# Memory attention of the sample group in the projection, and all sums of output weights made during the prompt attention

## The chip, the cores and the metric

The kernel runs on one core of one Trainium2 chip. The metric is device time in microseconds (us); before the change the median of three runs is 2398.44 us (2398.2 to 2399.28). The execution that was profiled took 2395.7 us.

## The reference

One mixer layer (DEPTH = 1) is computed for a prompt of 2048 tokens and for a sample group of 8 sequences with 4 new tokens each, from shared weights. All data is f32.

```python
D_MODEL, SEQ, DEC_BATCH, DEC_SEQ = 1024, 2048, 8, 4
SB_HEADS, SB_HEAD_DIM, MEM_HEADS, MEM_HEAD_DIM, N_MEM = 8, 64, 4, 128, 256
# h = rms_norm(x);  z = h @ w_in, split into column groups
# A  conv:   GLU -> causal depthwise conv (31) -> LayerNorm -> swish -> pointwise
# B  pool:   causal means over 2/4/8/16 minus the token, small matmul, scale
# C  stick-breaking attention: a = beta_k * prod over later k' of (1 - beta_k'), out = a @ v
# D  cross-attention into 256 memory tokens: softmax(q k^T / sqrt(128)) @ v
# each group output * silu(its gate);  concat @ w_out;  rms_norm;  + x
```

The change concerns group D of the sample group (its keys and values come from `cache_mem_k` and `cache_mem_v`, 256 tokens by 512 columns for each of the 8 sequences) and the product with `w_out` (2048 x 1024).

## The kernel before

**Stages.** There are three, one after the other on the tensor engine (PE):

- The *projection* (until about 1478 us) computes `z = h @ w_in` in two halves of the columns, part 0 and part 1. Every f32 operand is split into a high and a low fp32r piece, and three products are summed (`xhi*whi`, `xlo*whi`, `xhi*wlo`, L243). Beside it, PE works through the stick-breaking attention of the sample group on the paged cache (L987, L1026), whose pages GpSimd (POOL) fetches by indirect DMA (L941). Side tasks are added to `tasks` in `main` (L1865) and give PE a little work between the products.
- The *prompt attention* (`sb_prompt`, L1293, about 1478 to 1937 us) runs over `hp` (4 pairs of heads), `qb` (4 blocks of 512 queries) and `kc` (blocks of 512 keys from `qb` down to 0). For each block, PE makes scores `S` (L1271); ScalarE (ACT) makes two sigmoids, `gam` (L1275) and `be` (L1276); VectorE (DVE) scans `E` (L1341, L1344); POOL multiplies `be` by `E` (L1353); PE transposes the result into `AT` (L1364); DVE or ACT copies it to `at` (L1368 on the diagonal, L1370 elsewhere); PE multiplies it with `V` into `av` (L1380). The scan's second operand `ZM` is in PSUM (L1300, L1905).
- The *output stage* (about 1937 to 2394 us) computes `concat @ w_out` with a Strassen-like scheme of seven products, in the order 1, 7, 2, 6, 4, 5, 3 (`parts`). Each product takes eight weight tiles of 128x512. For products 7, 6, 5 and 4 such a tile is a sum or difference of blocks of `w_out`, made on POOL (`weight_sum`, L1615). Then ACT makes the high piece (`wohi`, L1621), DVE the low one (`wolo`, L1626; POOL for product 1). On the other side, blocks of the mixer output `mr` are combined (L1699 to L1706) and split into `mh` and `ml` (L1714, L1725). PE accumulates them into `acc` (L1968). The tail of the conv group (`conv_post`, L1444 to L1514: layer norm, swish, pointwise product `cz` at L1511 from `shi` and `slo`, gate `cgt` at L1514) is interleaved there.

**Group D of the sample group.** `sample_keys` (L440) runs as a task in part 0: for each of 8 sequences it loads the keys, transposes them on PE (`smt`, L453), copies them from PSUM on ACT (L454) and stores them to `mkTd` in DRAM. `sample_mem` (L1147) runs as the first side work of the prompt attention: it loads them again (`mkbT`, L1174) with the values (`mvb`, L1168), makes scores `smS` (L1181), a softmax, transposes of the probabilities (`smpt`, L1205), products with the values (`smO`, L1220), picks each head's columns with a mask (`smOm` and `smR` on DVE, L1223 and L1227), transposes back (`smr`, L1231) and stores its part of the mixer output (L1237). `sample_end` (L1079 to L1144) finishes the sample group's stick-breaking attention behind it.

**What sets the order.** PE's order is written by hand (`manual_schedule`): a block's transposes follow its scores by a fixed number of steps, and side work is taken between steps by a budget of cost. The orders of ACT, DVE, POOL and of the DMA issues on SyncE (SP) are made by a tile scheduler when the program is built, which may hoist an instruction far ahead of where the source has it. Each engine executes its own order strictly; an instruction whose input isn't ready holds up all behind it on its engine.

`side_work` (L1927) is the list of what is done beside the prompt attention: `sample_mem`, `sample_end`, the weights of product 1 (`out_weights`, L1629), the first mixer blocks, and the start of the conv tail. In the output stage, `out_weights(prod, pool, engine, lead, ...)` loads weight tiles `lead` steps ahead of their use.

## Time and profile before

| what | value |
|---|---|
| median of 3 runs | 2398.44 us (2398.2 to 2399.28) |
| profiled execution | 2395.7 us, its span 2394.0 us |
| PE busy | 2275.1 us (95%) |
| DVE, POOL, ACT busy | 1732.6, 1286.6 and 1117.0 us (72%, 54% and 47%) |
| mean granted PE clock | 0.986 |
| DMA traffic | 562.14 MB, mean 235 GB/s |

The span is the time between the first and the last instruction on record; the execution's own time is 1.7 us longer. The times of stages are read in us from the span's start. A row of a waits view has the waiting engine and line, what released it, and total, count and longest of these waits. In a timeline row stand start, duration, engine, line, operation and tiles, and in brackets the idle time of the engine ahead of it with its releaser. In a windows row, each engine's busy time within the stretch is followed by the number of its instructions; then come granted clock, busy share of the DMA engines, and GB/s.

### The profile page before, as it was taken

What the parts mean: (1) busy time and instruction counts of PE and PEld (TensorE: products, weight loads), DVE (VectorE), ACT (ScalarE), POOL (GpSimd) and SP (SyncE); (2) the same over time, 40 slices, a digit from 0 to 9 for tenths busy, and PEclk for the clock granted to TensorE, in tenths of its full rate; (3) what the DMA queues carried; (4) which work ended last, traced back from release to release, by engine and by line L of the source; (5) the groups of instructions that cost most, each with busy time, mean ns of one, the idle gap of its engine ahead of it and who ended that gap; (6) DMA issues with size and microseconds to landing.
All of it is one profiled execution on the core that took longest, in us unless ns stands there. A gap on an engine that the chain in (4) does not pass through costs nothing. (4 is left out here: it accounts for less than half of the span.)

```text
span 2394.0 us, 42116 instructions
## 1 busy us (share of the span) xinstructions
PE 2275.1 (95%) x15962; PEld 1769.7 (74%) x15962; DVE 1732.6 (72%) x2420; ACT 1117.0 (47%) x1939; POOL 1286.6 (54%) x1323
## 2 busy tenths in 40 slices
PE   7899999999999999999999999899999998989996
PEld 7888888898888777777777776455555557778775
DVE  5332785959756764587877878879898846687998
ACT  5322343242442322224242435788989955443554
POOL 3454535556464655546556554667776754454430
PEclk9999999999999999999999999999999999999998
DMA  6678988887778899978878767834333217887764
GB/s 211 196 253 290 347 287 309 305 269 267 259 256 306 301 357 318 318 270 276 272 268 274 260 222 190 238 77 119 82 93 80 63 63 250 268 284 239 255 236 164
DMA packets 340437, 562.14 MB, mean 235 GB/s; under 512 B 28481, under 2 KB 212929, under 8 KB 323834
## 3 DMA queue, kind: packets, MB, share of 16 engines
q1 hardware_dynamic: 284858, 290.72, 39.2%
q0 software_dynamic: 55376, 268.72, 31.6%
q8 instruction: 126, 2.06, 0.3%
q14 instruction: 77, 0.63, 0.1%
HBM read 469.28 MB, written 90.68 MB: 234 GB/s over the span
## 5 line engine op out<-in xcount | busy, mean ns | idle before, releaser
L974 DVE STREAM_TRANSPOSE T<-kt 128x1024 f32<-128x1024 f32 x256 | 308.5, 1225 | 184.1 <-PE sSA L987 179.4
L941 POOL DMA_INDIRECT vt<-in_cache_v_dram,idv x256 | 252.8, 988 | 255.1 <-PE sO L1026 194.3
L629 DVE SCALAR_TENSOR_TENSOR cacc<-U,par,cacc 128x512 f32<-128x512 f32 x480 | 360.2, 750 | 11.5
L1353 POOL TENSOR_TENSOR be<-be,E 128x512 f32<-128x512 f32 (+3 forms) x316 | 301.2, 960 | 106.1 <-DVE E L1344 45.9
L1344 DVE TENSOR_TENSOR_SCAN E<-gam,cr,ZM 128x513 f32<-128x513 f32 x192 | 233.0, 1264 | 14.8 <-ACT gam L1275 13.5
L941 POOL DMA_INDIRECT kt<-in_cache_k_dram,idk x128 | 128.1, 1001 | 194.3 <-DVE T L974 155.0
L1364 PEld LDWEIGHTS AT<-ident,be 128*128 128x128 f32 x1082 | 115.7, 141 | 128.1 <-ACT at L1370 45.1
L1968 PE MATMUL acc<-wohi,mh 128*128 128x512 f32 (+1 forms) x480 | 194.6, 405 | 2.1 <-DVE mh L1725 1.1
L1275 ACT ACTIVATE gam<-S,nbias_bc 128x1024 f32<-128x1024 f32 (+1 forms) x158 | 171.6, 1086 | 46.0 <-ACT be L1276 17.1
L1968 PE MATMUL acc<-wolo,mh 128*128 128x512 f32 (+1 forms) x480 | 190.8, 397 | 0.0
L1968 PE MATMUL acc<-wohi,ml 128*128 128x512 f32 x448 | 179.0, 400 | 9.8 <-DVE ml L1725 9.6
L1271 PE MATMUL S<-kT,Q 128*128 128x512 f32 (+1 forms) x632 | 175.2, 401 | 4.6 <-DVE sg1sg L727 2.4
L1276 ACT ACTIVATE be<-S,bias_bc 128x1024 f32<-128x1024 f32 (+1 forms) x158 | 170.7, 1080 | 0.0
L1364 PE MATMUL AT<-ident,be 128*128 128x128 f32 x1082 | 156.3, 282 | 15.0 <-DVE at L1368 3.9
L1380 PE MATMUL av<-at,V 128*64 128x512 f32 (+3 forms) x640 | 152.6, 555 | 1.7 <-DVE sbo L1385 1.7
L987 PE MATMUL sSA<-T,W 128*32 128x128 f32 x4096 | 138.4, 276 | 3.2 <-DVE T L974 2.4
L987 PEld LDWEIGHTS sSA<-T,W 128*32 128x32 f32 x4096 | 104.1, 110 | 40.0 <-issue 31.1
L1725 DVE TENSOR_TENSOR ml<-mr,mh 128x512 fp32r<-128x512 f32 x108 | 98.6, 918 | 35.0 <-ACT mh L1714 34.6
L1026 PE MATMUL sO<-vt,saT 128*32 128x512 f32 x1024 | 122.3, 593 | 0.0
L1271 PEld LDWEIGHTS S<-kT,Q 128*128 128x128 f32 x632 | 105.6, 194 | 19.7 <-ACT be L1276 3.4
L1370 ACT COPY at<-AT 128x512 f32<-128x512 f32 x192 | 109.5, 661 | 14.4 <-PE AT L1364 14.4
L1341 DVE TENSOR_TENSOR_SCAN E<-gam,ZM 128x384 f32<-128x384 f32 (+1 forms) x124 | 94.5, 812 | 24.8 <-ACT gam L1275 22.1
(581 smaller groups left out, 6044.3 us busy)
## 6 DMA issues: line engine op xcount, KB each, us to landing
Q<-qd SPq DMA_DIRECT2D x64, 256.0 KB
mr<-mixd SPq DMA_DIRECT2D x32, 512.0 KB
mr<-mixd SPq DMA_DIRECT2D x48, 256.0 KB
wor<-in_w_out_dram SPq DMA_DIRECT2D x20, 512.0 KB
xtp<-in_x_prompt_dram SPq DMA_DIRECT2D x16, 512.0 KB
kT<-kd SPq DMA_DIRECT2D x64, 128.0 KB
wor<-in_w_out_dram SPq DMA_DIRECT2D x32, 256.0 KB
msd<-mr SPq DMA_DIRECT2D x32, 256.0 KB
```

Of the source, the lines that this page charges most:

```text
L629: dve.scalar_tensor_tensor(out=ps, in0=U[:, a + k : a + k + H], scalar=wd[:, k : k + 1], in1=ps, op0=ALU.mult, op1=ALU.add)
L941: pool.indirect_dma_start(out=dst, out_offset=None, in_=rows, in_offset=bass.IndirectOffsetOnAxis(ap=idx, axis=0))
L974: S["turn"] = dve.transpose(T[:, 2 * hh : 2 * hh + 2].rearrange("p s j t -> p (s j t)"), kt[:, 2 * hh : 2 * hh + 2].rearrange("p s j d -> ...
L987: pe.matmul(sSs[n][32 * g : 32 * g + 32, P * ml : P * (ml + 1)], lhsT=W[:, jj, :], rhs=T[:, :, jj, :], start=i == 0, stop=i == 3, tile_pos ...
L1271: pe.matmul(S[:, j, :w], lhsT=Q[:, x, P * (q2 + j) : P * (q2 + j + 1)], rhs=kt[:, :w], start=x == 0, stop=x == 1)
L1275: act.activation(out=ga, in_=S[:, :, :w], func=AF.Sigmoid, bias=nbias_bc[:, h : h + 1], scale=-1.0)
L1276: act.activation(out=be, in_=S[:, :, :w], func=AF.Sigmoid, bias=bias_bc[:, h : h + 1])
L1344: dve.tensor_tensor_scan(out=E[:, j][:, ::-1], data0=g_[:, j][:, ::-1], data1=ZM[:, 0:1].to_broadcast([P, 513]), initial=carry[hh, q2][:, ...
L1353: pool.tensor_tensor(out=be[:, j, :m], in0=be[:, j, :m], in1=E[:, j, 513 - w : 513 - w + m], op=ALU.mult)
L1364: pe.transpose(ap_[:, P * qt : P * (qt + 1)], A[hp, qb, kc, hh, qt][:, P * r : P * (r + 1)], ident)
L1380: pe.matmul(av[64 * hh : 64 * hh + 64, c], lhsT=V[:, 4 * kc + r, 64 * hh : 64 * hh + 64], rhs=ats.pop((hp, qb, kc, r, hh))[:, c], start=dg ...
L1968: pe.matmul(o[:rows], lhsT=m[a][:, k, :rows], rhs=W[prod, 4 * h + k][w], start=not cont and h == k == n == 0, stop=h == 1 and k == 3 and n ...
```

## The change

Three things are changed.

1. `sample_keys`, its DRAM tile `mkTd` and the round trip through it are gone. `sample_mem` becomes a task of the projection's part 1. For each sequence it loads the keys, transposes them (8 transposes), copies them on ACT, and makes the scores at once (4 matmuls of 32x256, one to each strip of 32 columns of the array); DVE adds the result into `sc`. Then follow the softmax and, for each sequence, 4 matmuls with the values, a copy on ACT, and two small matmuls with a selection matrix `Sel` that pick the heads and transpose at once, in place of `smOm`, `smR` and `smr`.
2. The side work of the prompt attention now begins with `sample_end`. Behind it comes `weight_sums`: for each of 8 steps two loads of 512 KB, four sums of 128x512 on POOL and two stores of 512 KB to `wsd`. The weights of product 1 come after it.
3. In the output stage `weight_sum` is gone: products 7, 6, 5 and 4 load ready sums from `wsd`, two tiles in one transfer, and products 7 and 5 load two steps ahead in place of one.

```diff
-    mkTd = dram.tile([NB, P, 4, NMEM], F32, name="mkTd")
-    wsd = dram.tile([2, 8, P, 512], F32, name="wsd")
+    wsd = dram.tile([2, 8, P, 2, 512], F32, name="wsd")
...
-    def sample_keys():
-        for b in range(NB):
...
-            sp.dma_start(k_, cmk[b].rearrange("(t p) c -> p t c", p=P))
...
-            wq.dma_start(mkTd[b], kT)
...
+    def sample_mem():
+        while state["early"] < 6:
+            yield
...
+        ahead = yield from rows(cmk, 0, "mkb")
...
         for b in range(NB):
+            k_ = ahead
+            ahead = yield from (rows(cmk, b + 1, "mkb") if b + 1 < NB else rows(cmv, 0, "mvb"))
+            kT = k4(f"mkbT{b}", [P, 4, NMEM], F32)
+            for t in range(2):
+                pt = tp_tile(f"smt{b}_{t}")
...
+                    pe.transpose(pt[:, P * h : P * (h + 1)], k_[:, t, P * h : P * (h + 1)], ident)
+                act.copy(kT[:, :, P * t : P * (t + 1)], pt.rearrange("p (h n) -> p h n", h=4))
+                yield
+            yield
+            S = tp_tile(f"smS{b}")
+            for h in range(4):
+                pe.matmul(S[32 * h : 32 * h + 32, :NMEM], lhsT=qm[:, b, h, :], rhs=kT[:, h, :], start=True, stop=True,
+                          tile_position=(0, 32 * h))
+            if b:
                 dve.tensor_tensor(out=sc, in0=sc, in1=S[:, :NMEM], op=ALU.add)
...
+        for b in range(NB):
+            k, g = divmod(b, 4)
...
+            O = tp_tile(f"smO{b}")
             for t in range(2):
+                for c in range(2):
+                    r = 64 * t + 32 * c
+                    pe.matmul(O[r : r + 32, :256], lhsT=pv[:, t, g], rhs=v_[:, t, 256 * c : 256 * c + 256], start=True,
+                              stop=True, tile_position=(0, r))
+            Os = small(f"smOs{b}")
+            act.copy(Os[:, :256], O[:, :256])
...
+            for n in range(2):
+                pe.matmul(pt[:, 2 * TS * n : 2 * TS * (n + 1)], lhsT=Os[:, P * n : P * (n + 1)],
+                          rhs=Sel[:, k, n].rearrange("p c q -> p (c q)"), start=True, stop=True)
...
         sp.dma_start(mixs[3], mo)
...
+    def weight_sums(wsp):
+        ts = {}
+        for j in range(9):
+            if j < 8:
+                ts[j] = [wsp.tile([P, 2, 512], F32, tag="ws", name=f"ws{j}_{n}", bufs=6) for n in range(2)]
+                for t, r in zip(ts[j], half_rows(j)[::-1]):
+                    sp.dma_start(t.rearrange("p b n -> p (b n)"), w_out0[r])
+            yield
+            if j:
+                t, u = ts.pop(j - 1)
+                for o, a, b, op_ in ((t[:, 1], t[:, 1], u[:, 1], ALU.subtract), (u[:, 1], u[:, 1], u[:, 0], ALU.subtract),
+                                     (u[:, 0], t[:, 1], u[:, 0], ALU.add), (t[:, 0], t[:, 0], u[:, 0], ALU.subtract)):
+                    pool.tensor_tensor(out=o, in0=a, in1=b, op=op_)
+                    yield
+                for n, o in enumerate((t, u)):
+                    sp.dma_start(wsd[n, j - 1], o)
+                yield
...
-    def weight_sum(prod, j, ts):
-        store()
-        if len(ts) == 2:
-            pool.tensor_tensor(out=ts[0], in0=ts[0], in1=ts.pop(), op=ALU.add if prod == 6 else ALU.subtract)
...
+        if prod in SUMS:
+            two = wsd[n, j : j + 2, :, h]
...
+        sp.dma_start(slot, two.rearrange("b p n -> p b n"))
+        seconds[prod, j + 1] = slot[:, 1]
...
-        yield from z_groups(0, GROUPS[0][12:14])
-        tasks.add(sample_keys())
-        yield from z_groups(1, GROUPS[1][:-2])
+        yield from z_groups(1, GROUPS[1][:7])
+        tasks.add(sample_mem())
+        yield from z_groups(1, GROUPS[1][7:-2])
...
-        for i, part in enumerate((sample_mem, sample_end)):
-            with tc.tile_pool(name=f"sm{i}", bufs=1, side="left", reuse_waits="tile") as sm2:
-                yield from part(sm2, side_ps, S)
+        with tc.tile_pool(name="sm", bufs=1, side="left", reuse_waits="tile") as sm2:
+            yield from sample_end(sm2, side_ps, S)
+        with tc.tile_pool(name="wsp", bufs=1, side="left", reuse_waits="tile") as wsp:
+            yield from weight_sums(wsp)
...
-        yield from spread(out_weights(7, op, dve, 1, wr), 2 * LEAD, 1.5)
+        yield from spread(out_weights(7, op, dve, 2, wr), 2 * LEAD, 1.5)
...
-                               fourth(), spread(out_weights(5, opm, dve, 1, wr), at((2, 8, 0)) - 1, 1),
+                               fourth(), spread(out_weights(5, opm, dve, 2, wr), at((2, 8, 0)) - 1, 1),
```

How the orders move is seen at three places. In the names below, `be_3_3_0_2` is the tile `be` of `qb` 3, `kc` 3, head 0 of the pair, query tiles 2 and 3; `ws_0` and `ws_1` are the two halves of the rows of `w_out` in `weight_sums`. First POOL in the prompt attention, at the blocks of `qb` 2 of the second pair of heads, now (L1575 is the new sum; `be` is at L1335, `cr` at L1331):

```order
L1335 TENSOR_TENSOR be_2_2_1_2_16585<-be_2_2_1_2_16585,E_2_2_1_2_16654 128x511
L1575 TENSOR_TENSOR ws_0_17258<-ws_0_17258,ws_1_17259 128x512
L1575 TENSOR_TENSOR ws_1_17259<-ws_1_17259 128x512
L1575 TENSOR_TENSOR ws_1_17259<-ws_0_17258,ws_1_17259 128x512
L1575 TENSOR_TENSOR ws_0_17258<-ws_0_17258,ws_1_17259 128x512
L1335 TENSOR_TENSOR be_2_1_0_0_16616<-be_2_1_0_0_16616,E_2_1_0_0_16685 128x512
L1331 COPY cr_2_1_0_0_16688<-E_2_1_0_0_16685 128x2
L1335 TENSOR_TENSOR be_2_1_0_0_16616<-be_2_1_0_0_16616,E_2_1_0_0_16685 128x512
L1335 TENSOR_TENSOR be_2_1_0_2_16651<-be_2_1_0_2_16651,E_2_1_0_2_16717 128x512
```

Before, the `be` of block 2_2 was followed by that of block 2_1 at once. Now four sums stand between them. Another four in a row stand ahead of the next `be` but two, and four ahead of a `be` of the first pair's `qb` 3; the other twenty stand singly or in groups of two or three, from the first pair's `qb` 3 to here. Second, POOL at the start of the output stage, before (`pwlo`, `csq` and `cs` belong to the conv tail):

```order
L1615 TENSOR_TENSOR wor_0_20039<-wor_0_20039 128x512
L1615 TENSOR_TENSOR wor_1_20042<-wor_1_20042 128x512
L1542 TENSOR_TENSOR pwlo<-pwr_20078,pwhi 128x512
L1615 TENSOR_TENSOR wor_2_20087<-wor_2_20087 128x512
L1463 TENSOR_TENSOR csq_0_20202<-csq_0_20202,csq_1_20205 128x256
L1615 TENSOR_TENSOR wor_3_20149<-wor_3_20149 128x512
L1463 TENSOR_TENSOR csq_2_20208<-csq_2_20208,csq_3_20211 128x256
```

and now:

```order
L1524 TENSOR_TENSOR pwlo<-pwr_20202,pwhi 128x512
L1445 TENSOR_TENSOR csq_0_20317<-csq_0_20317,csq_1_20320 128x256
L1445 TENSOR_TENSOR csq_2_20323<-csq_2_20323,csq_3_20326 128x256
L1445 TENSOR_TENSOR csq_0_20317<-csq_0_20317,csq_2_20323 128x256
L1433 TENSOR_TENSOR cs_20507<-cy_20293 128x256
```

The sums have left this stretch, and the conv tail's work follows without them. Third, PE in part 1 of the projection, now (`z1q` is a column group of `z`):

```order
L242 MATMUL z1q_0_9968<-xlo,whi1q_9812 128x512
L242 MATMUL z1q_0_9968<-xhi,wlo1q_9811 128x512
L1172 MATMUL smS_10042<-mkbT_9906,qm 32x256 x4
L1166 MATMUL smt_0_10051<-ident,mkb_9904 128x128 x4
L242 MATMUL z1q_1_10057<-xhi,whi1q_9812 128x512
L242 MATMUL z1q_1_10057<-xlo,whi1q_9812 128x512
```

The scores of one sequence and the first transposes of the next stand between two column groups. Behind the end of `sample_end`, PE's order is the same in both kernels up to the last instruction.

More of the change, by code (lines that the diff above doesn't have):

```diff
@@ L1161, in sample_mem @@
-        for g in (2, 3):
-            pool.tensor_tensor(out=hm, in0=hm, in1=h4[:, g], op=ALU.add)
-        sc = sm.tile([P, NMEM], F32, name="smsc", bufs=1)
-        kb = {}
-        def load(b):
-            t = sm.tile([P, 2, 512], F32, tag="mkb", name=f"mvb{b}", bufs=8)
-            sp.dma_start(t, cmv[b].rearrange("(t p) c -> p t c", p=P))
-            return t
-        kT = []
+        rest = zc.tile([P, 2, NMEM], F32, tag="ps", name="smrest", bufs=1)
+        sc = rest[:, 0]
+        pT = rest[:, 1].rearrange("p (t g h k q) -> p t g h k q", t=2, g=4, h=4, k=2)
@@ new lines, in sample_mem, with rows @@
+        Sel = zc.tile([P, 2, 2, 2, TS], F32, name="msel")
+        pool.memset(Sel, 0.0)
+        for k in range(2):
+            for t in range(2):
+                pool.affine_select(out=Sel[:, k], in_=Sel[:, k], compare_op=ALU.not_equal, fill=1.0, base=-64 * t - 4 * k,
+                                   pattern=[[-8, 2], [-48, 2], [-1, TS]], channel_multiplier=1)
+        def rows(src, b, nm):
+            while state["att"]:
+                yield
+            t = k4(f"{nm}{b}", [P, 2, 512], F32)
+            sp.dma_start(t, src[b].rearrange("(t p) c -> p t c", p=P))
+            return t
@@ L1643, in out_weights @@
             if j < 8:
-                weight_sum(prod, j, ts[j])
+                store()
             if j + lead < 8:
```

143 lines of the change are left out of this document (45 added, 98 removed).

## The prediction

> **What bounds the kernel now.** I read the page first. PE is nearly always busy:
>
> ```profile
> PE 2275.1 (95%) x15962; PEld 1769.7 (74%) x15962; DVE 1732.6 (72%) x2420; ACT 1117.0 (47%) x1939; POOL 1286.6 (54%) x1323
> PE   7899999999999999999999999899999998989996
> PEclk9999999999999999999999999999999999999998
> ```
>
> No other engine comes near, and the average says little about a change that shifts work between stages. So the windows view is next, at the stages that gain or lose work (busy us of PE, PEld, DVE, ACT, POOL, then the granted clock and the DMA share):
>
> ```profile
> 1100.00:1200.00 100.00, 100.00 (x750) 74.07 (x749) 72.81 (x93) 24.13 (x42) 53.18 (x49) 1.00 0.83 283
> 1480.00:1500.00 20.00, 14.78 (x74) 9.66 (x74) 15.76 (x24) 13.56 (x16) 12.36 (x21) 0.74 1.01 280
> 1500.00:1550.00 50.00, 44.70 (x282) 24.99 (x276) 43.02 (x62) 37.71 (x44) 30.04 (x38) 0.97 0.78 228
> 1550.00:1600.00 50.00, 47.58 (x280) 26.80 (x278) 42.00 (x49) 42.11 (x58) 38.01 (x58) 1.00 0.36 91
> 1600.00:1650.00 50.00, 45.46 (x273) 27.15 (x272) 42.14 (x69) 41.03 (x57) 29.91 (x43) 1.00 0.48 115
> 2000.00:2050.00 50.00, 41.95 (x205) 34.44 (x204) 35.88 (x64) 27.30 (x54) 26.03 (x24) 0.90 0.88 291
> 2100.00:2150.00 50.00, 42.73 (x214) 36.00 (x213) 43.25 (x63) 21.33 (x40) 27.52 (x22) 0.93 0.87 279
> 2200.00:2250.00 50.00, 44.46 (x184) 34.26 (x183) 42.91 (x51) 22.97 (x48) 33.51 (x21) 0.97 0.76 256
> ```
>
> Three regimes are seen. In part 1 of the projection PE has no idle time: work added there is paid in full. The prompt attention has PE, DVE, ACT and POOL all at 60 to 95%, coupled in one chain of blocks; its start is the worst stretch, with PE at 14.8 of 20 us and a clock of 0.74. The output stage has holes in PE's row, and its clock falls beside them. So I asked for PE's waits in the output stage, in the stretches 2000 to 2050, 2100 to 2160 and 2160 to 2240:
>
> ```profile
> PE cz L1511 <- ACT shi L1487: 6.6, 1, 6.6
> ...
> PE cz L1511 <- DVE cgt L1514: 7.0, 2, 3.7
> ...
> PE acc L1968 <- DVE ml L1725: 5.5, 4, 3.2
> ```
>
> The longest is 6.6 us at 2012. The timeline in front of it shows whose delay it is:
>
> ```profile
> 2013.45 0.62 ACT L1621 CAST wohi<-wor 128x512 fp32r<-128x512 f32 x1 [3.54 <-POOL wor L1615]
> ...
> 2014.11 0.69 DVE L1626 TENSOR_TENSOR wolo<-wor,wohi 128x512 fp32r<-128x512 f32 x1 [1.87 <-ACT wohi L1621]
> ...
> 2015.02 1.26 POOL L1615 TENSOR_TENSOR wor<-wor 128x512 f32<-128x512 f32 x1 [1.59 <-DMA wor<-in_w_out_dram]
> 2016.31 0.62 ACT L1621 CAST wohi<-wor 128x512 fp32r<-128x512 f32 x1 [1.23 <-POOL wor L1615]
> 2016.83 0.83 ACT L1481 ACTIVATE csg<-ct,par 128x256 f32<-128x256 f32 x2
> 2017.34 0.88 DVE L1485 SCALAR_TENSOR_TENSOR ct<-ct,par,csg 128x256 f32<-128x256 f32 x2 [2.54 <-ACT csg L1481]
> 2018.17 0.64 ACT L1487 CAST shi<-ct 128x256 fp32r<-128x256 f32 x2
> ...
> 2112.59 0.62 ACT L1621 CAST wohi<-wor 128x512 fp32r<-128x512 f32 x1 [2.75 <-POOL wor L1615]
> ```
>
> A weight block lands late, POOL sums it late, ACT stands 3.54 and then 1.23 us at `wohi` in its fixed order, and `csg`, `ct` and `shi`, which have nothing to do with weights, come behind it; PE waits for `shi`. The sum is on the path that sets the end here. In the other two places a sum is one of several causes: DVE has 43 of 50 us of work, and at 2112 (the last row) `wohi` also stood 2.75 us behind a sum.
>
> **The change, part by part.** The groups of the instructions concerned (first all of the run's PE groups; then the sums, and `wolo` on DVE, in the output stage; then `wolo` on POOL in the attention):
>
> ```profile
> L1181 PE MATMUL smS<-mkbT,qm 128*32 128x256 f32 x64 | 4.7, 400 | 3.4 <-DMA mkbT<-mkTd 1.8 <-DVE at L1368 1.6
> L1220 PE MATMUL smO<-mvb,smpT 128*32 128x512 f32 x32 | 3.8, 598 | 0.7 <-ACT at L1370 0.7
> L453 PE MATMUL smt<-ident,mkb 128*128 128x128 f32 x64 | 9.6, 272 | 0.0
> L1205 PE MATMUL smpt<-ident,smp 128*128 128x128 f32 x2 | 0.4, 300 | 0.8 <-DVE at L1368 0.8
> ...
> L1615 POOL TENSOR_TENSOR wor<-wor 128x512 f32<-128x512 f32 x30 | 43.6, 1456 | 44.2 <-DMA wor<-in_w_out_dram 22.2 <-DMA wor<-wsd 15.5 <-issue 2.4
> ...
> L1626 DVE TENSOR_TENSOR wolo<-wor,wohi 128x512 fp32r<-128x512 f32 x48 | 46.7, 988 | 17.4 <-ACT wohi L1621 16.7
> ...
> L1626 POOL TENSOR_TENSOR wolo<-wor,wohi 128x512 fp32r<-128x512 f32 x8 | 10.3, 1283 | 0.0
> ```
>
> *Projection.* The transposes `smt` (9.6 us) leave part 0 and enter part 1; PE's digits are nines in both, so they cancel. New in part 1 are `smS` (4.7), `smO` (3.8) and `smpt` (0.4), 8.9 us, and sixteen small matmuls with `Sel`. The trace has none of 128x8; the nearest row is `smpt`, 0.2 us each, so 3.2 us. The bounds are half and twice that (a narrow moving operand, or a full pass for each): 1.6 to 6.4. Stalls come on top: PE stands still if a copy on ACT, the `sc` sum on DVE or a load is late when its turn in the fixed order comes. ACT has 24 of 100 us of work there and DVE 73, and several groups of products lie between a transpose and its scores, so I take 1 us; the bound below is none, above it one stall of 0.5 us for each of the 16 sequence steps, 8. Two table loads for the exponential fall on ACT, which has room. DMA, at 0.83 there, gets 8 MB of keys and values (16 loads of 512 KB, 8 of which come over from part 0), while 8 MB of `mkTd` traffic vanishes. Projection: +13 us (10.5 to 23).
>
> *Start of the attention.* The same `smS`, `smO`, `smpt` leave it (8.9 us), and `smr`'s two transposes (0.6). So do their waits, from PE's waits in 1480 to 1530 and 1530 to 1600:
>
> ```profile
> PE smS L1181 <- DMA mkbT<-mkTd: 1.8, 3, 0.6
> PE AT L1364 <- DVE smsc L1184: 1.6, 1, 1.6
> PE smS L1181 <- DVE at L1368: 1.6, 1, 1.6
> ...
> PE AT L1364 <- DVE smOm L1223: 1.3, 1, 1.3
> PE smpt L1205 <- DVE at L1368: 0.8, 1, 0.8
> PE smO L1220 <- ACT at L1370: 0.7, 1, 0.7
> ```
>
> That is 7.8 us. The low clock of 1480 to 1500 and of 1500 to 1550 costs 20 x 0.26 + 50 x 0.03 = 6.7 us, but part of it follows the first wait of the stage, which stays; I take 2. Sum: 9.5 + 7.8 + 2 = 19 us gained (9.5, if every wait only changes its name, to 24).
>
> *Sums in the attention.* POOL gets 32 sums. In the attention a POOL operation of the same form took 1.28 us (`wolo`, 1283 ns), so 41 us; at the output stage's 1.456 it would be 47. By the order of POOL they stand among the `be` of `qb` 3 of the first pair up to `qb` 2 of the second, about 1545 to 1660 in the trace of before. POOL has 38.0 + 29.9 = 67.9 of 100 us of work in 1550 to 1650: with 41 it is 109. So POOL is over-full there by some 9 us, or 15 at the higher price. What is queued behind a sum is the next `be`, and behind that PE's `AT`, which has little slack: in the attention as a whole PE's weight loads wait for `be` 32 times already, and at 1580 `be` ended 2.3 us before the transposes that read it were due:
>
> ```profile
> PEld AT L1364 <- POOL be L1353: 25.4, 32, 1.8
> ...
> 1571.22 1.28 DVE L1344 TENSOR_TENSOR_SCAN E<-gam,cr,ZM 128x513 f32<-128x513 f32 x1 [0.54 <-ACT gam L1275]
> ...
> 1578.95 1.09 POOL L1353 TENSOR_TENSOR be<-be,E 128x512 f32<-128x512 f32 x1
> 1579.31 1.28 DVE L1344 TENSOR_TENSOR_SCAN E<-gam,cr,ZM 128x513 f32<-128x513 f32 x1
> ...
> 1582.38 0.42 PEld L1364 LDWEIGHTS AT<-ident,be 128*128 128x128 f32 x4 [0.30 <-issue]
> ```
>
> Four sums in a row are 5.1 us, 2.8 more than that slack. I take the 9 us of overflow and 2 for a second such place, 11; the bounds are 3 (one place alone) and 25 (overflow of 15 plus five places at 2). The loads and stores (16 MB) find DMA at 0.36 to 0.48 and cost nothing as long as SP isn't held; a store on SP waits for its sum, with loads of `kT` and `Q` behind it, and the 11 includes no price for that. Attention: -19 + 11 = -8 us (-21 to +15).
>
> A rule of the Trainium skill (page "SBUF — State Buffer", section "Who interferes with whom") bears on both homes of the sums: a VectorE instruction with two operands in SBUF and a GpSimd instruction that reads SBUF block each other. Here `wolo` on DVE, 0.69 us at its quickest in the rows above, averages 988 ns in the output stage, and sums average 1456 there, which agrees. By it, the scans of the attention would be locked out too if both operands lay in SBUF; `ZM` is in PSUM, and of the two scans just quoted the one beside `be` on POOL took 1.28 us like the one without. So I charge DVE nothing in the attention.
>
> *Output stage.* Gone are the 32 sums with their waits. At 2012, 6.6 us: `wohi` then waits for a load alone, issued two tiles ahead and early. I take 6; if the load is late all the same, nothing. At 2104 and 2112 (7.0 us) the `cgt` in front of `cz` sits behind stretched `wolo` on DVE and the other operations on `mr`, which stay: half, 3.5. At 2218 (5.5 us with its neighbours) `ml` sits behind two `wolo` and a `wohi` that waited for a sum: 4. The clock loses 50 x (0.10 + 0.07 + 0.03) = 10 us in the three windows; it falls beside these holes, so it recovers with them: 8. Output: -22 us (-8, if all but the 2012 hole is handed to the next operation on DVE, with its clock loss; to -32, the sum of all these waits, 19.1, and the clock, 10, and some 3 of smaller ones).
>
> The Trainium skill (page "TensorE: Matmul & The Clock Gate", part "The HAM clock gate") says that an idle window of about 3.4 us halves PE's clock. The windows above, with 0.90 beside the 6.6 us hole, agree. By it, the four holes of 3 us and more cost at least half of such a window each, 4 x 1.7 = 6.8 us, an estimate; with it the sum would be a microsecond higher.
>
> Sum: 2395.7 + 13 - 8 - 22 = 2378.7 us. The profiled execution lies 2.7 below the median of the runs, 2398.44. So I predict 2381 us.
>
> **Rivals.**
>
> *POOL bounds the attention* (slower side). Sums and `be` run on one in-order engine, where two sides of a block must pass through it. If the stalls repeat at every place where sums stand ahead of `be`, and if PE's holes there cross the length after which the clock falls, the 11 becomes 25 + 8 = 33; with the projection at its upper end (+23), the total is +23 - 19 + 33 - 22 = +15, about 2413. It decides from the point where sums cost the attention more than 28 us (11 + 17). For it: 109 of 100 us, and waits for `be` already on record. Against: PE's order puts a block's transposes six steps behind its scores, 1600 to 1650 alone had 20 us of idle time on POOL, and stalls on `AT` delay the next `be` too, so that one backlog is paid once.
>
> *The output stage hands its waits on.* DVE is at 43 of 50 us there, and what waited for a sum then waits for DVE. Gain 8 in place of 22: 2395, slightly better than before. For it: two of the three holes are DVE's. Against: the 2012 hole is POOL's and ACT's alone.
>
> *The projection pays more.* Stalls at their upper bound (+23 in place of +13): 2391. For it: DVE at 73 us of 100 and three shared PSUM buffers for transposes and scores. Against: PE has no idle time in these rows with similar side tasks in it.
>
> *Full relief.* Sums cost 3, the output stage yields 32: 2395.7 + 13 - 16 - 32 = 2360.7, with the 2.7 2363. For it: DVE is freed as well from the stretched `wolo`.
>
> *The load of a ready sum lies late* (the change does not do what it says): ACT waits for `wsd` as it did for POOL. DMA is at 0.88 there; but the change cuts traffic in this stage. It is a part of the second rival.
>
> **How the numbers follow.** Forecast 0.42; POOL bound 0.20; waits handed on 0.14; projection dearer 0.12; full relief 0.12. A measurement of this kernel can tell 0.2% (4.8 us) from no change. The forecast and full relief are faster; of the second and third rivals (0.26), 0.11 lie within 0.2%, 0.13 below and 0.02 above; the first is slower but for 0.02 within. Faster 0.67, same 0.13, slower 0.20. The range goes from 2361 (full relief) to 2404 (the milder half of the POOL case); the forecast's own is 2370 to 2392.
>
> **What would show it.** Right: PE's wait of 6.6 us at `cz` for `shi` is gone, and the granted clock between 2000 and 2250 is above 0.96; part 1 of the projection is some 12 us longer with PE still full; PE's waits for `smS`, `smO`, `smpt` in the attention are gone. The price of the sums shows as PE waits at `AT` for POOL in the second to seventh block-rows of the attention, about 11 us. It is wrong if those exceed 28 us, if projection and output stage merely exchange their waits, or if DVE's scans lengthen beside the sums.

## The result, and the profile after

The changed kernel takes 2387.73 us (median of 6 runs, 2384.94 to 2390.53), the kernel before 2398.32 us in the same comparison. The ratio is 0.9947, with a 95% interval from 0.9933 to 0.9961: faster by half a per cent, about 11 us where 17 were forecast. The time lies in the forecast's own range, 2370 to 2392 us. The profiled execution took 2387.03 us, its span 2385.3 us. The page of the changed kernel, PE's busy time and POOL's in 40 slices, and below it POOL's slices before:

```profile
PE 2283.3 (96%) x16024; PEld 1774.9 (74%) x16024; DVE 1717.9 (72%) x2428; ACT 1120.3 (47%) x1947; POOL 1282.7 (54%) x1322
...
POOL 3454545555565555545546462699877763531231
```

```profile
POOL 3454535556464655546556554667776754454430
```

PE is busier by 8 us and the run shorter by 9. POOL's load has moved from the last quarter to the 27th to 29th slice.

A stage's limits can be read from the first and last start of the score matmuls. The view of one source line gives them, before and now:

```profile
L1271 PE MATMUL S<-kT,Q x632: 277/397/796, 1480.0 to 1931.9; 128*128 128x512 f32 x128, 128*128 128x256 f32 x30
```

```profile
L1253 PE MATMUL S<-kT,Q x632: 276/397/797, 1490.9 to 1945.4; 128*128 128x512 f32 x128, 128*128 128x256 f32 x30
```

So the projection grew by 10.9 us. The attention, from first to last score, went from 451.9 to 454.5, where 8 us less had been forecast. The output stage, from the last score to the end, went from 462.1 to 439.9. These three make up the whole difference of the spans, 8.7 us: +10.9 + 2.6 - 22.2.

The windows of the changed kernel where sums arrived and where they left (PE, PEld, DVE, ACT, POOL, granted clock, DMA share, GB/s):

```profile
1550.00:1600.00 50.00, 44.86 (x232) 26.41 (x234) 40.11 (x53) 39.23 (x51) 45.23 (x52) 0.93 0.64 202
...
2000.00:2050.00 50.00, 45.76 (x226) 37.82 (x224) 35.38 (x61) 24.10 (x46) 22.19 (x19) 0.93 0.83 268
...
2100.00:2150.00 50.00, 42.95 (x218) 35.27 (x219) 38.44 (x64) 19.29 (x41) 21.06 (x18) 0.97 0.67 205
...
2200.00:2250.00 50.00, 50.00 (x221) 40.21 (x220) 43.52 (x61) 26.42 (x53) 19.01 (x12) 1.00 0.79 275
```

POOL now stands at 45 of 50 us in the attention, and the clock, which had been 1.00 there, at 0.93. In the output stage the clock went from 0.90, 0.93 and 0.97 to 0.93, 0.97 and 1.00 in the same windows, which now hold work of some 13 us earlier in the stage, since the stage begins that much later. PE's longest waits in the output stage were, before, and are now:

```profile
PE cz L1511 <- DVE cgt L1514: 11.7, 4, 3.7
PE acc L1968 <- DVE ml L1725: 9.6, 9, 3.2
PE cz L1511 <- ACT shi L1487: 7.3, 2, 6.6
```

```profile
PE cz L1493 <- ACT shi L1469: 8.8, 4, 4.1
PE acc L1959 <- DVE ml L1715: 4.1, 5, 1.8
...
PE cz L1493 <- DVE cgt L1496: 1.7, 1, 1.7
```

The hole of 6.6 us at `cz` has not closed, only shrunk to 4.1, and all waits for `shi` together rose from 7.3 to 8.8 us. It is the waits for `cgt` and `ml` that became short. The waits view of ACT in that stage, before and now, says why:

```profile
ACT wohi L1621 <- POOL wor L1615: 53.3, 25, 6.1
```

```profile
ACT wohi L1611 <- DMA wor<-in_w_out_dram: 19.2, 7, 5.0
ACT wohi L1611 <- DMA wor<-wsd: 9.6, 6, 3.1
```

`wohi` no longer waits for POOL, but for loads, most of all those of product 2, which was never a sum: 12.2 of the 19.2 us are four waits from 2020 to 2050. The first of them, 3.2 us, is in front of the hole of 4.1 us.

### The profile page after: what moved, and what is told of

The parts are those of the page before. It is cut to its first block, busy times and chain, and to the rows that moved or that the text cites. A ratio compares the mean times of both kernels' runs of the same rounds, so it can differ in the third digit from the quotient of the medians.

```text
span 2385.3 us, 42238 instructions
## 1 busy us (share of the span) xinstructions
PE 2283.3 (96%) x16024; PEld 1774.9 (74%) x16024; DVE 1717.9 (72%) x2428; ACT 1120.3 (47%) x1947; POOL 1282.7 (54%) x1322
## 5 line engine op out<-in xcount | busy, mean ns | idle before, releaser
L1335 POOL TENSOR_TENSOR be<-be,E 128x512 f32<-128x512 f32 (+3 forms) x316 | 300.7, 963 | 70.0 <-DVE E L1326 22.5
L1326 DVE TENSOR_TENSOR_SCAN E<-gam,cr,ZM 128x513 f32<-128x513 f32 x192 | 233.3, 1264 | 23.3 <-ACT gam L1257 13.9
L1346 PE MATMUL AT<-ident,be 128*128 128x128 f32 x1082 | 161.4, 286 | 20.9 <-DVE at L1350 9.1
L1715 DVE TENSOR_TENSOR ml<-mr,mh 128x512 fp32r<-128x512 f32 x108 | 87.2, 812 | 30.7 <-ACT mh L1704 30.6
```

Of the source, the lines that this page charges most:

```text
L1326: dve.tensor_tensor_scan(out=E[:, j][:, ::-1], data0=g_[:, j][:, ::-1], data1=ZM[:, 0:1].to_broadcast([P, 513]), initial=carry[hh, q2][:, ...
L1335: pool.tensor_tensor(out=be[:, j, :m], in0=be[:, j, :m], in1=E[:, j, 513 - w : 513 - w + m], op=ALU.mult)
L1346: pe.transpose(ap_[:, P * qt : P * (qt + 1)], A[hp, qb, kc, hh, qt][:, P * r : P * (r + 1)], ident)
```

## The experiments

Each run is compared with the kernel before on the same chip. The table splits the profiled execution of each at the first and last score start, in us. "Attention and output" is the sum of the two, since side work can move across the border between them. The lengths are those of one execution each; the projection, in the six traces in which it is that of the kernel before, takes 1476.2 to 1484.6 us. So differences of a few us between two rows say nothing.

| kernel | ratio (95%) | projection | attention | output | attention and output |
|---|---|---|---|---|---|
| before | 1 | 1480.0 | 451.9 | 462.1 | 914.0 |
| changed | 0.9947 (0.9933 to 0.9961) | 1490.9 | 454.5 | 439.9 | 894.4 |
| memory attention moved alone | 0.9996 (0.9982 to 1.0009) | 1490.0 | 439.8 | 463.2 | 903.0 |
| sums moved alone | 0.9942 (0.9926 to 0.9959) | 1476.2 | 468.4 | 430.8 | 899.2 |
| changed, sums left out | 0.9912 (0.9896 to 0.9929) | 1486.1 | 438.4 | 447.7 | 886.1 |
| changed, twice the sums | 1.0121 (1.0088 to 1.0155) | 1491.2 | 490.7 | 440.6 | 931.3 |
| sums in part 0 | 1.0070 (1.0053 to 1.0088) | 1522.3 | 439.8 | 444.5 | 884.3 |
| changed, lead 1 | 0.9941 (0.9919 to 0.9963) | 1488.4 | 454.9 | 438.5 | 893.4 |
| sums alone, lead 1 | 0.9915 (0.9898 to 0.9933) | 1482.0 | 467.8 | 428.6 | 896.4 |

**The two halves of the change apart.** First the memory attention alone, with the weights of the kernel before (`e1`), then the sums alone (`e2`):

```diff
 # e1: the changed kernel, without weight_sums, with weight_load, weight_sum and lead of the kernel before
-        with tc.tile_pool(name="wsp", bufs=1, side="left", reuse_waits="tile") as wsp:
-            yield from weight_sums(wsp)
 # e2: the kernel before, with weight_sums, weight_load and lead of the changed kernel
         for i, part in enumerate((sample_mem, sample_end)):
...
+        with tc.tile_pool(name="wsp", bufs=1, side="left", reuse_waits="tile") as wsp:
+            yield from weight_sums(wsp)
```

> Only the memory attention of the sample group is moved into the projection; the 32 sums of weights stay on POOL in the output stage. If the prediction's terms hold (projection +13, start of the attention -19, output stage unchanged), 2398.4 - 6 = 2392 us, and the attention from first to last score is some 440 us against 458 before. If the stage gains less because other waits take the place of the removed ones (rival: -12), 2399 us and an attention of 446 us. The output stage keeps its length, 462 us from the last score to the end, and its wait of about 6.6 us for shi at cz.

> Only the sums of weights are moved into the prompt attention, behind sample_mem and sample_end, which stay there. Theory of the prediction: attention +11, output -22, together 2387 us. Rival (the sums cost the attention 19, as its unchanged length in the changed kernel would have it if the removal of sample_mem gained the full 19): 2395 us. The output stage is some 440 us from the last score to the end in both.

The memory attention alone is worth nothing that can be measured: 0.9996. Its projection is 10 us longer and its attention 12.1 us shorter. The sums alone have the whole gain: 0.9942 against 0.9947 for the full change. Their attention is 16.5 us longer and their output stage 31 us shorter. So the whole gain comes from one half of the change. The price in the attention, 16.5, lies between my 11 and the rival's 19, nearer to the rival; the total is still lower than I expected (2379.76 us, with the kernel before at 2395.28), since the output stage gained more than in the changed kernel.

Beside the sums, the move of the memory attention gains less than alone. Attention and output together fall by 11 us with it where the sums stay in the output stage (914.0 to 903.0), but by 3 to 5 where the sums are in the attention (899.2 to 894.4; with the shorter lead 896.4 to 893.4). The projection's price is paid in both cases.

**The price of the sums.** In `e3` the four sums in `weight_sums` are left out, in `e6` one more into a scratch tile goes ahead of each:

```diff
 # e3: the step's yields stay, and plain blocks of w_out are stored
-                    pool.tensor_tensor(out=o, in0=a, in1=b, op=op_)
 # e6
+                    pool.tensor_tensor(out=wsp.tile([P, 512], F32, tag="extra", name=f"extra{j}_{op_}", bufs=1), in0=a, in1=b, op=op_)
                     pool.tensor_tensor(out=o, in0=a, in1=b, op=op_)
```

> The changed kernel without the 32 sums on POOL in the prompt attention; loads and stores of 16 MB stay, and what is stored are plain blocks of w_out, so the output differs. Theory (sums cost 11 in the attention): 2377 us, attention 447 us from first to last score. Rival (19): 2369 us, 439 us. If the 16 MB of transfers rather than the sums are what costs, it stays at 2388.

> The changed kernel with 32 more sums of the same form on POOL in the prompt attention, one into a scratch tile ahead of each. Without sums the attention took 438.4 us from first to last score, with 32 sums 454.5. If the sums' price is a queueing delay that grows in proportion (theory: about 15 us for 32, half of it PE idle time and half low clock), 64 sums give 468 to 472 us and 2402 us in all. If POOL becomes the bound of these blocks (rival), each further sum costs its full 1.29 us, +41 us: 495 us and 2429 us. If POOL's gaps hide the second sum, 456 us and 2389 us.

Without sums the attention takes 438.4 us, though all 16 MB of transfers are there: the transfers cost nothing, the 32 sums 16.1 us. By the attention this is the rival's case (439 us), by the total the theory's (11 us cheaper than the changed kernel): the ratio falls by 0.0035, some 8 us, since the output stage of `e3` is 7.8 us longer than that of the changed kernel. The next 32 cost 36.2 us more, 1.13 us for each sum of 1.28 us. The windows of `e6` show POOL as the bound:

```profile
1600.00:1650.00 50.00, 38.37 (x186) 22.23 (x187) 26.94 (x29) 31.85 (x46) 49.37 (x53) 0.83 0.47 142
```

POOL has 49.4 of 50 us of work, and PE, DVE and ACT fall together. The rival that I gave 0.20 was right for the second helping of sums. With POOL at 45 of 50 us, the changed kernel seems to stand just ahead of the point from which POOL decides.

How such a price comes together is seen by comparing PE's busy time in the attention of `e1`, which has no sums there, and of the changed kernel:

```profile
1490.00:1929.80 439.80, 413.52 (x2307) 242.28 (x2306) 386.93 (x480) 394.31 (x514) 329.53 (x436) 0.99 0.35 94
```

```profile
1490.90:1945.40 454.50, 421.18 (x2307) 246.75 (x2306) 387.95 (x480) 396.16 (x514) 367.90 (x468) 0.97 0.46 128
```

The same 2307 matmul records take 413.5 us in one and 421.2 in the other. Of 14.7 us, 7.0 are idle time of PE and 7.7 are the same work at a lower clock. Not all of it belongs to the sums: 72 us into the stage, where the first sum runs (1563), the changed kernel has 322 of these records done and `e1` 333, about 2 us behind, and its clock up to there is 0.91 against 0.95. PE's waits in the changed kernel's attention agree with the idle time (in `e1` those for POOL's `be` are 0.7 us):

```profile
PE AT L1346 <- DVE at L1350: 9.1, 10, 1.5
PE AT L1346 <- POOL be L1335: 7.8, 10, 1.2
PE S L1253 <- ACT be L1258: 4.8, 2, 3.0
```

**Where the sums stand.** Three edits of their place. `e5` makes them as a task of part 0, `e13` (with the memory attention in its old place) in the later half of part 1 with the loads further ahead, and `e8`, made from `e2`, puts the weights of product 1 ahead of them:

```diff
 # e5
+        tasks.add(weight_sums())
         yield from z_groups(0, GROUPS[0][14:])
 # e13, with 12 yields between load and sum in place of 3
+        tasks.add(weight_sums())
+        yield from z_groups(1, GROUPS[1][14:-2])
 # e8, with 4 buffers in place of 6
         opm = ox.enter_context(tc.tile_pool(name="opm", bufs=1, side="left", reuse_waits="tile"))
         yield from out_weights(1, opm, pool)
+        with tc.tile_pool(name="wsp", bufs=1, side="left", reuse_waits="tile") as wsp:
+            yield from weight_sums(wsp)
```

> The changed kernel with the sums of weights (loads, sums on POOL, stores) made as a side task of part 0 of the projection, where sample_keys had been, in place of the attention. Theory (POOL has room there and PE's order hides it): as without sums, 2377 us, with a projection within 2 us of the changed kernel's. Rival: POOL's sums delay the page fetches behind them, and DMA at 0.8 to 0.9 delays loads, so PE waits in the projection for T and xhi by 5 us or more: 2382 to 2390.

> All 32 sums moved out of the output stage, here into the later half of part 1 of the projection, with their loads asked for twelve task steps ahead in place of three; the memory attention stays in the prompt attention. Making the sums in part 0 had cost the projection 36 us, and its trace showed POOL waiting 7.7 us for a weight load with a page fetch queued behind it. If that wait was the cause (theory), the projection is now within 5 us of before (1480), the attention 452 and the output stage about 432, in all 2369 us or a ratio of 0.985 to 0.989. If the DMA engines' load is the cause (rival), PE waits in the projection for fetched pages again, 15 us or more, and the ratio is 0.995 or above.

> The kernel with only the sums moved into the attention, and there the weights of product 1 put ahead of the sums, four buffers in place of six. In POOL's order the sums then stand mostly in ones and twos ahead of a be, with one group of four, where the kernel it is made from had eight groups of three and four. If what costs is the length of a group ahead of a be (theory), the price of the sums falls from 16.5 us in the attention to about 8, and the ratio to before from 0.994 to 0.991. If it is POOL's load as such (rival), the ratio stays at 0.994.

`e5` is slower, 1.0070. The attention has the 439.8 us of a kernel without sums there, but the projection is 31 us longer than the changed kernel's. Of these, 18 are idle time of PE and 13 the same work at a lower clock (0.93 in 300 to 480, against 1.00). Two kinds of wait in 300 to 480 make up the idle time, one for the transposed keys `T`, five for fetched values `vt`:

```profile
PE sSA L970 <- DVE T L957: 10.7, 1, 10.7
PE sO L1009 <- DMA vt<-in_cache_v_dram,idv: 7.9, 5, 2.4
```

The timeline in front of the long one:

```profile
308.42 1.29 POOL L1852 TENSOR_TENSOR ws<-ws,ws 128x512 f32<-128x512 f32 x1 [7.69 <-DMA ws<-in_w_out_dram]
...
322.06 0.46 SPq L594 DMA_DIRECT2D mixd<-po  x1
...
331.51 0.62 DVE L591 SCALAR_TENSOR_TENSOR po<-py,par,sg0pg 128x384 f32<-128x384 f32 x1 [10.64 <-DMA mixd<-po]
...
333.60 2.32 DVE L957 STREAM_TRANSPOSE T<-kt 128x1024 f32<-128x1024 f32 x2
...
336.07 1.29 PE L970 MATMUL sSA<-T,W 128*32 128x128 f32 x20 [10.68 <-DVE T L957]
```

POOL stood 7.7 us before a sum whose weights had not landed. The stores of these sums, and the loads behind them, which waited 4.3 us for the stores to free a buffer, held up SP's order until 322, and with it a store of `po` that was computed at 314. That store landed about 9 us later; from 318 to 330 the DMA engines were busy for 0.98 of the time, at 381 GB/s. DVE stood 10.6 us for it, with `T` behind, and PE for `T`. No page fetch was late here: DVE did not wait for one before `T`. So the recorded reading of this trace, which `e13` below builds on, names the wrong queue: what was held up was SP's, and the load on the DMA engines had its part. This run can't tell how much each of the two had.

`e13` (0.9998; lead 1) has a projection of 1484.0 us, within the 5 us of the theory. But 12 of its 32 sums had not run by then, and it differs from `e5` in more than the lead of the loads, so it doesn't settle what was wrong there. It lost the gain elsewhere: its attention takes 473.5 us, with nothing of the sums intended in it. POOL's timeline at the change of stages:

```profile
1486.79 1.27 POOL L1870 TENSOR_TENSOR ws<-ws,ws 128x512 f32<-128x512 f32 x1 [27.73 <-DMA ws<-in_w_out_dram]
...
1504.04 2.60 POOL L1870 TENSOR_TENSOR ws<-ws,ws 128x512 f32<-128x512 f32 x2
1506.58 0.52 POOL L1297 MEMSET zm<- 128x512 f32 x1
```

```profile
PE S L1271 <- ACT be L1276: 22.6, 3, 21.7
```

The last three groups of four sums slid past the end of the projection, behind a load that POOL waited 27.7 us for; the mask `zm`, without which the attention can't go on, came behind them. ACT, which copies it to `ZM`, stood 19.8 us for it, and PE 21.7 us for ACT. Without that wait the run would be near the 2369 us that I expected, but that was not tried.

`e8` did not bear out my theory of the long groups: 0.9965 (0.9946 to 0.9984), no better than `e2`. Its sums stand mostly in ones and twos, but earlier, beside `sample_mem`, and the attention takes 478.3 us against 468.4. POOL isn't fuller there. First a window of `e8`, then one of `e2`, each where sums stand:

```profile
1550.00:1600.00 50.00, 41.56 (x220) 23.14 (x218) 34.06 (x40) 35.61 (x48) 43.95 (x50) 0.90 0.64 210
```

```profile
1650.00:1700.00 50.00, 41.64 (x214) 24.21 (x212) 34.47 (x39) 36.95 (x47) 48.86 (x54) 0.86 0.63 199
```

What differs is that POOL waits in `e8` for loads of sums, 5.8 us in all (1.0 in `e2`). The longest such wait, 4.4 us, ends at 1580, and from 1584 to 1592 PE waits 3.41, 1.80 and 1.92 us for `be`. The four buffers in place of six may have made these loads late. So `e8` changes more than the grouping, and it shows neither that long groups are harmless nor what sets the price.

**How many sums.** From the kernel before, only the sums of product 7 (`e10`), or of products 7 and 6 (`e11`), are made in the attention; the others stay in the output stage. Product 7 loads two steps ahead in both:

```diff
-    FACTORS = {1: (11,), 7: (22, 12), 2: (21,), 6: (0, 11), 5: (12, 11), 4: (21, 1), 3: (22,)}
+    FACTORS = {1: (11,), 7: (0,), 2: (21,), 6: (0, 11), 5: (12, 11), 4: (21, 1), 3: (22,)}   # e10
+    FACTORS = {1: (11,), 7: (0,), 2: (21,), 6: (1,), 5: (12, 11), 4: (21, 1), 3: (22,)}      # e11
```

> The kernel before, but the 8 sums of product 7 alone are made in the prompt attention (8 loads of 512 KB, 8 sums, 8 stores of 256 KB) and loaded ready in the output stage; the other 24 sums stay there, and so does the memory attention. The price of sums in the attention was found to grow faster than their number (16 us for 32, 36 more for the next 32). Theory: 8 sums cost the attention 2 us or less, the hole of 6.6 us at the start of product 7 and its low clock go (-8 to -11): ratio 0.996 to 0.997. Rival: the output stage only gains when all sums are gone: 1.000.

> As the run before it, with the 8 sums of product 6 made in the attention too, 16 in all. Theory: 16 sums cost the attention 4 to 6 us, and the output stage gains 15 to 20 of the 22 us that all 32 gained: ratio 0.994 to 0.995. Rival (a gain from each further sum is eaten by its price): as with 8 sums.

The ratios are 0.9980 (0.9967 to 0.9994) and 0.9976 (0.9965 to 0.9987). The attention takes 456.5 and 459.1 us, the output stage 458.7 and 448.8. But the profiled execution of `e10` took 2401.59 us, the longest of its twelve (median 2393.97), so its stages are too long and can't be set beside its ratio. That of `e11` (2390.2, median 2392.37) can: 16 sums cost 7.2 us in the attention where 32 cost 16.5 (`e2`), about half a microsecond each, and the output stage gives 13.3 us for 16 and 31.3 for 32. So price and gain go roughly with the number. My theory of a price that grows faster held only beyond 32. The hole at product 7 was not worth 8 us by itself: by the medians the 8 sums bring 4.5 us, price included. In `e10` no wait for `shi` is 6.6 us long any more, but PE's waits for `ml` and `shi` are longer in total than before (9.6 and 7.3):

```profile
PE acc L1985 <- DVE ml L1740: 16.2, 11, 3.3
PE cz L1511 <- ACT shi L1487: 10.9, 5, 3.5
```

In `e11` they are 10.6 and 8.3 us. That is the rival of the waits that are handed on.

**The lead.** In `e9` (from the changed kernel) and `e12` (from `e2`), products 7 and 5 load one step ahead again:

```diff
-        yield from spread(out_weights(7, op, dve, 2, wr), 2 * LEAD, 1.5)
+        yield from spread(out_weights(7, op, dve, 1, wr), 2 * LEAD, 1.5)
...
-                               fourth(), spread(out_weights(5, opm, dve, 2, wr), at((2, 8, 0)) - 1, 1),
+                               fourth(), spread(out_weights(5, opm, dve, 1, wr), at((2, 8, 0)) - 1, 1),
```

> The changed kernel with the loads of products 7 and 5 issued one step ahead, as before the change, in place of two. If the lead matters, wohi on ScalarE waits for the load and the hole at cz near the start of product 7 returns to 6 us or more, +3 to +8 us in the output stage (2392 to 2396 us). If the pair transfers alone bring it, the time stays at 2388 within 3 us.

> All 32 sums moved into the attention, the memory attention left where it was before, and the loads of products 7 and 5 one step ahead as before. As the lead did not matter in the changed kernel, the ratio is that of the sums alone, 0.994; if the lead costs something it is 0.992.

The longer lead brings nothing: 0.9941 with lead 1 against 0.9947. `e12`, the sums alone with lead 1, has the lowest ratio of the kernels that compute the whole result, 0.9915 (0.9898 to 0.9933). Its interval touches that of the changed kernel only at the edge. It came out as I had written for the case that the longer lead costs something, but it overlaps with that of `e2` (0.9926 to 0.9959), so such a cost isn't shown.

**The shared port.** The prediction charged DVE nothing for sums in the attention, since the scans' second operand is in PSUM. `e7` moves the operand of the 192 long scans to SBUF:

```diff
+        zs = sb.tile([P, 8], F32, name="zs", bufs=1)
+        pool.memset(zs, 0.0)
...
-                                               data1=ZM[:, 0:1].to_broadcast([P, 513]), initial=carry[hh, q2][:, j, :],
+                                               data1=zs[:, 0:1].to_broadcast([P, 513]), initial=carry[hh, q2][:, j, :],
```

> The changed kernel with the second operand of the 192 long scans on VectorE (a broadcast zero) taken from SBUF in place of PSUM; the sums on POOL stay. By the Trainium skill (page SBUF - State Buffer, section Who interferes with whom), a VectorE instruction with two operands in SBUF and a GpSimd instruction that reads SBUF lock each other out: by it, scans beside POOL's work would lengthen from 1.26 us to 1.8 us or more, and with DVE at 40 to 45 of 50 us the attention would grow by 30 us or more. If a broadcast single element does not use the shared port, scans stay at 1.26 us and the time at the changed kernel's.

The ratio is 1.0453 (1.0415 to 1.0490), and the attention 560.4 us. First the groups of the changed kernel, then those of `e7`, in the attention:

```profile
L1326 DVE TENSOR_TENSOR_SCAN E<-gam,cr,ZM 128x513 f32<-128x513 f32 x192 | 233.3, 1264 | 23.3 <-ACT gam L1257 13.9
...
L1575 POOL TENSOR_TENSOR ws<-ws,ws 128x512 f32<-128x512 f32 x24 | 30.8, 1286 | 1.5 <-DVE E L1323 0.5
```

```profile
L1328 DVE TENSOR_TENSOR_SCAN E<-gam,cr,zs 128x513 f32<-128x513 f32 x192 | 350.6, 1874 | 28.2 <-ACT gam L1257 12.7 <-POOL be L1337 11.6 <-ACT be L1258 3.8
...
L1577 POOL TENSOR_TENSOR ws<-ws,ws 128x512 f32<-128x512 f32 x24 | 41.5, 1730 | 1.1
L1325 DVE TENSOR_TENSOR_SCAN E<-gam,ZM 128x512 f32<-128x512 f32 x32 | 38.2, 1193 | 0.0
```

One operand of four bytes in a partition, in SBUF in place of PSUM, lengthens scans from 1264 to 1874 ns and sums from 1286 to 1730 ns. The 32 scans of 128x512 in the same run, whose operand is still in PSUM (the last row), take 1193 ns, and 1195 in the changed kernel. The rule of the Trainium skill (page "SBUF — State Buffer", section "Who interferes with whom") holds here, for scans and for a broadcast too. It is one reason for the attention as a home for the sums: in the output stage a sum had taken 1456 ns. No run here shows what share of the gain comes from it.

## Why the prediction was right or wrong, point by point

*What bounds.* Right. Up to the first score PE's busy time rose by 17.1 us (from 1440.6 to 1457.7), and the output stage's holes were the place of the gain.

*Projection, +13.* Measured +10.9 in the profiled pair. PE's groups there are somewhat dearer than estimated:

```profile
L1172 PE MATMUL smS<-mkbT,qm 128*32 128x256 f32 x64 | 5.1, 391 | 0.0
...
L1206 PE MATMUL smO<-mvb,smrest 128*32 128x256 f32 x64 | 5.1, 391 | 0.0
L1215 PE MATMUL smr<-msel,smOs 128*128 128x8 f32 x32 | 4.0, 235 | 0.0
```

With `smpt` (0.4) that is 14.6 us against 12.1; the small matmuls with `Sel` cost 4.0 against 3.2. There was no stall at any of them. Yet the projection grew by less than they add up to, since PE's idle time in it fell by 6.2 us, from 39.4 to 33.2. My term counted the work that comes and no idle time that goes. Over the six traces with the memory attention there and a projection otherwise like the changed kernel's (1486.1 to 1491.2) and the six with that of the kernel before (1476.2 to 1484.6), the means differ by 8.7 us, less than my lower bound of 10.5.

*Start of the attention, -19.* This step failed. `e1` shows -12.1 (and `e3` -13.5): PE's busy time fell by 10.2, from the 423.75 of the next row (the kernel before) to 413.52, and its idle time by 1.9 where I had taken 7.8.

```profile
1480.00:1931.90 451.90, 423.75 (x2406) 246.47 (x2406) 392.28 (x495) 395.31 (x513) 329.71 (x439) 0.98 0.40 109
```

The step was "So do their waits". They did go, but they had covered waits of the blocks themselves. The waits of the kernel before, and of `e1`, in the attention:

```profile
PE AT L1364 <- DVE at L1368: 3.9, 4, 1.2
...
PE S L1271 <- ACT be L1276: 2.2, 3, 1.3
...
PE av L1380 <- DVE sbo L1385: 1.7, 7, 0.3
```

```profile
PE AT L1346 <- DVE at L1350: 7.5, 10, 1.2
PE S L1253 <- ACT be L1258: 4.8, 2, 3.0
PE av L1362 <- DVE sbo L1367: 3.6, 8, 1.9
```

These three grew from 7.8 to 15.9 us, 8.1 more, as much as went, and 6.4 of the 8.1 lie in the first 110 us of the stage, where the memory attention had been. So the chain of a block seems no shorter when PE has less beside it; PE waits for the chain instead. The lower bound of that term, 9.5, had named this case, and the truth lay nearer to it.

*Sums in the attention, +11.* The mechanism was right, POOL nearly full and `be` late, the size too small: 14.7 us against `e1`, 16.1 against `e3`, 16.5 in `e2` against the kernel before. My overflow of 9 us with a place or two more counted PE's idle time alone, which rose by 7.0. As much again, 7.7, came from the lower clock (0.97 for 0.99 over the stage). I had priced the clock in the output stage, and in the rival, but not in this term.

*Output stage, -22.* Measured -22.2, partly for other reasons than I gave. The windows of the whole stage, before and now:

```profile
1931.90:2394.00 462.10, 410.73 (x1916) 327.78 (x1914) 348.94 (x567) 220.16 (x486) 181.73 (x142) 0.95 0.69 228
```

```profile
1945.40:2385.30 439.90, 404.44 (x1916) 323.87 (x1914) 333.81 (x567) 218.40 (x486) 138.15 (x110) 0.97 0.65 211
```

PE lost 15.9 us of idle time and 6.3 of busy time, the same 1916 records at a higher clock; I had taken 13.5 and 8. Within the idle time the shares were others. I expected 6 of the 6.6 us hole at `cz` back and got 2.5, since `wohi` of product 2 now waits for its load there, and the waits for `shi` in total even rose; the waits for `cgt` gave 10 (11.7 to 1.7) and those for `ml` 5.5 (9.6 to 4.1), more than the 3.5 and 4 that I took. That the sum came out to 0.2 us is in part luck: the output stage differs by 8 us between `e3` and the changed kernel, which have the same order in it.

*Rivals.* POOL bounds the attention: not with 32 sums, but with 64 (`e6`). Waits are handed on: so for 8 sums (`e10`), and for 4.1 of the 6.6 us at 2012. A dearer projection: no. Full relief: not as a whole, but the output stage of the sums alone yields its 31 us (`e2`). The load of a ready sum lies late: in part, `wohi` waits 9.6 us for `wsd`. That the full change isn't needed, and that one half of it earns nothing, was none of my rivals.

*In all.* The forecast's gain was 7 us too large by the medians. In the profiled pair, with `e1` beside it, the start of the attention gained 6.9 us less than its term and the sums cost 3.7 more, the projection cost 2.1 less, and the output stage agreed. Of the named signs, the clock from 2000 to 2250 (0.97) and the lost waits for `smS`, `smO` and `smpt` came; the wait for `shi` at `cz` stayed, shorter.

What stays open: the changed kernel and `e3` have the same order of instructions in the output stage, and their profiles differ by 8 us there (439.9 and 447.7); `e2`, with another order, has 430.8. In general this stage takes 429 to 434 us in the four kernels that have all sums out of it and the memory attention in its old place, and 438 to 450 in the six that have the sums out of it and the memory attention moved. I didn't find what sets this.

## What to carry to other kernels

A wait that is taken off the bounding engine is a gain only if the chain behind it is ready; look for the next releaser of the same instruction before counting it. Work put on a half-idle in-order engine is not free: here a sum of 1.28 us cost about half a microsecond. And a piece that waits for a load stops everything queued behind it, be it a store on SP or a mask that a whole stage needs. Of a change with two halves, run each alone: here one earned everything.

## What the runs showed of the hardware that was not expected

PE's clock falls without any long hole. In 1550 to 1600 of the changed kernel PE's longest wait is 1.46 us, yet the clock there is 0.93. The timeline at 1589 shows what it follows, a cluster of short waits at `AT`:

```profile
1590.94 0.96 PE L1346 MATMUL AT<-ident,be 128*128 128x128 f32 x6 [1.46 <-DVE at L1350]
...
1592.62 0.47 PE L1346 MATMUL AT<-ident,be 128*128 128x128 f32 x1 [0.72 <-POOL be L1335]
```

Behind two waits, of 1.46 and 0.72 us, the single `AT` already takes 0.47 us. At another place of the same trace a single `AT` behind a wait takes 0.33:

```profile
1674.56 0.33 PE L1346 MATMUL AT<-ident,be 128*128 128x128 f32 x1 [1.18 <-POOL be L1335]
```

There it took four waits, of 1.18, 0.85, 0.72 and 0.85 us, until an `AT` took 0.47 (1677.96). So no number of waits can be read from this, but waits are to be counted by how close they lie as well as by length: over this attention, 7.0 us of added idle time came with 7.7 us lost to the clock.
